# A decoder layer on one core: one key operation moved from VectorE to ScalarE, keys copied out of PSUM first, a branch and the tail's transposes placed elsewhere

## The chip, the cores and the metric

The kernel runs on one core of one Trainium2 chip. The metric is the device time of one execution in microseconds (us). The core has five engines with a queue each: PE (TensorE, matrix products and transposes), DVE (VectorE), ACT (ScalarE), POOL (GpSimd) and SP (SyncE, which here issues DMA transfers). An engine takes its instructions in the order of its own queue and waits at an instruction until what that instruction depends on is done. Matmuls write into PSUM, which has eight banks of 128 x 512 floats; DVE and ACT read them from there into SBUF.

## The reference, cut to what matters

```
h = rmsnorm(x);  proj = h @ w_in       # 512 tokens, D = 1024
# branch A: 8 heads, keys from a latent of rank 128, an indexer keeps the top 128 keys per query
o_a = sparse_attention(q_a, rmsnorm(c_kv) @ w_uk, w_uv, indexer(q_idx, k_idx, w_idx), rel_bias)
# branch B: 8 heads, stick-breaking attention
z = q_b . k_b * scale; a = exp(log_sigmoid(z) + suffix_sum(log_sigmoid(-z))); o_b = a @ v_b
x = x + (sigmoid(gate_a) * (o_a @ w_branch_a) + sigmoid(gate_b) * (o_b @ w_branch_b)) @ w_out
# 32 experts of width 256, 2 per token
h2 = rmsnorm(x); x = x + sum_e comb[:, e] * (silu(h2 @ w_gate[e]) * (h2 @ w_up[e])) @ w_down[e]
x = x + (p @ w_ple) * sigmoid(rmsnorm(x) @ w_ple_gate)
return rmsnorm(x)                      # all float32
```

## The kernel before, in words

Precision is kept by splitting: a float32 array is stored as a rounded part (hi) and a remainder (lo), and a product is three matmuls, hi·hi, lo·hi and hi·lo (`mm3`, lines L80 to L82). A weight block of 1024 columns is loaded by SP (`wraw`), rounded by POOL (`whi`, L130), and its remainder is made by DVE (`wlo`, L134).

From about 20 to 330 us the program goes through projections (`FILLS`): blocks named kb, qb (keys and queries of branch B, `kpl` and `qpl` after the copy from PSUM), qa, g (the branch gates, copied from PSUM by ACT as `gst`, L443), and the up-projections uk and uv. Each fill is 24 matmuls into one bank of a pair (`pj`, two banks in turn). Between the fills stand pieces of attention: scores `z_ps` (L491, L493) and suffix sums (L526) of branch B, logits `lg_ps` (L575, L576) of branch A, and the indexer's selection of top keys on DVE (MAX8 and MATCH_REPLACE8, L379 and L380). The order is the order of the code, laid out by hand and placed on each engine's queue by the scheduler.

A head's keys are stored stacked by `stack_k` (L291 to L298), `ks`: 64 partitions hold the head's hi, the other 64 the same hi, for slice 0; slice 1 holds the lo on both halves. It makes four operations of 64 x 512: two copies on ACT (L294, L295) and two subtractions on DVE (L296, L297), all four read from the source. It is called once for the indexer's keys (from PSUM), for the 8 heads of branch B (from `kpl`, in SBUF), and by `a_stack` (L548 to L552) for the 8 heads of branch A, two heads a call, directly from the PSUM bank `ka_ps`. That bank belongs to the `pj` pair, so the next fill but one writes it again. The four `a_stack` calls stand at about 152, 188, 228 and 269 us; the fill that takes the bank next is the qb fill at the first and a gate fill at the last.

From 442 us the mixture of experts runs as 16 pairs of experts. For each, POOL gathers 128 token rows by an indirect DMA (`xg`), PE transposes them (L1016), ACT scales them (`xT`), and PE multiplies by gate and up weights (`gu_ps`, L1031, 16 matmuls), transposes `hid`, multiplies by the down weights (`yp`, L1054) and adds the result to the tokens (`cmb_ps`, L1065, L1066). SP loads the weights `ew` ahead (L702, L704), as their buffers come free. `overflow` (L1071) is a branch at run time: it holds the work for experts with more tokens than the slots, and is jumped over when there are none (as with these inputs). Every engine loads the count into a register, compares and jumps; the join waits for the engine's own work. In the kernel before it stands inside the last pair's gate and up product, after 8 of 16 matmuls.

From 700 us the tail multiplies the normed tokens by `w_ple_gate` (`gate_x3`, four token tiles by two halves), applies the sigmoid (`sg`), adds to `x` and normalizes; `turn_h3` transposes a tile (`h3T`).

Of the kernel before, what the change touches and what calls it, by code (L numbers as in the profile page):

```python
# [49 lines left out]
def hybrid_layer_kernel(ctx: ExitStack, tc: tile.TileContext, x, p, attn_norm, w_in, kv_norm, w_uk, w_uv,  # L50
# [25 lines left out]
    def ov(name):  # L76
        return bank(7, name)
# [213 lines left out]
    def stack_k(src, r0):  # L291
        k = att.tile([P, 2, S], F32R, tag="ks", bufs=3, name="ks")
        o0 = 64 - r0
        nc.scalar.activation(k[r0:r0 + 64, 0], src[r0:r0 + 64], AF.Copy)  # L294
        nc.scalar.activation(k[o0:o0 + 64, 0], src[r0:r0 + 64], AF.Copy)  # L295
        V.tensor_sub(k[r0:r0 + 64, 1], src[r0:r0 + 64], k[r0:r0 + 64, 0].bitcast(F32))  # L296
        V.tensor_sub(k[o0:o0 + 64, 1], src[r0:r0 + 64], k[r0:r0 + 64, 0].bitcast(F32))  # L297
        return k  # L298

    onehot = tmp("onehot")  # L300
# [247 lines left out]
    def a_stack(pr):  # L548
        ka = pj("ka_ps")
        uk = late["uk"]  # L550
        mm3(ka, [uk[:, i, pr * P:(pr + 1) * P] for i in range(2)], late["cs"])
        sa[pr] = ([stack_q(heads["qa", pr], 64 * hh) for hh in range(2)], [stack_k(ka, 64 * hh) for hh in range(2)])  # L552

    def a_bias(u):
        pr, qb = u // 4, u % 4
# [316 lines left out]
    def sm(*shape):  # L872
        small[0] += 1
        return mo.tile([P, *shape], F32, name=f"sm{small[0]}")
# [124 lines left out]
    ple_part(3, 1)  # L999


    st_ = {}

    def pair_in(i):
        g_ = xg[i % 2]
        st_[i] = {}
        st_[i]["in"] = nc.gpsimd.indirect_dma_start(out=g_, out_offset=None, in_=h2_d,  # L1007
                                     in_offset=bass.IndirectOffsetOnAxis(ap=trow[:, i:i + 1], axis=0),
                                     bounds_check=S - 1, oob_is_err=False)
        gk = g_.rearrange("s (p k) -> s k p", k=KD)  # L1010
        xT = []
        for half in range(2):
            xT.append(xp.tile([P, 4, P], F32, tag="xT", bufs=4, name="xT"))
            tp = at("xg_ps")
            for k in range(4):
                nc.tensor.transpose(tp[:, k * P:(k + 1) * P], gk[:, 4 * half + k, :], ident)  # L1016
            for k in range(4):
                kk = 4 * half + k
                nc.scalar.activation(xT[half][:, k, :], tp[:, k * P:(k + 1) * P], AF.Copy, scale=gpm[:, kk:kk + 1])  # L1019
        hT_ = mo.tile([P, S], F32R, tag="hotT", bufs=2, name="hotT")  # L1020
        V.tensor_scalar(hT_, iota_t, tokf[:, i:i + 1], None, op0=ALU.is_equal)
        st_[i].update(xT=xT, hot=hT_, y={})

    def pair_gu(i, between=None):
        xT = st_[i]["xT"]
        gu_ps = pj("gu_ps")
        for k in range(KD):
            if between and k == KD // 2:
                between()
            for e in range(2):  # L1030
                nc.tensor.matmul(gu_ps[64 * e:64 * e + 64, :], xT[k // 4][:, k % 4, 64 * e:64 * e + 64],  # L1031
                                 wq[i, k // 4][:, :, e * D + (k % 4) * 256:e * D + (k % 4 + 1) * 256], start=k == 0, stop=k == KD - 1)
        hid = mo.tile([P, 256], F32, tag="hid", bufs=2, name="hid")
        nc.scalar.activation(hid, gu_ps[:, :256], AF.Silu)  # L1034
        V.tensor_mul(hid, hid, gu_ps[:, 256:])  # L1035
        st_[i]["hid"] = hid
# [23 lines left out]
    def pair_out(i, nh, ts=range(NT)):  # L1060
        yh, yl = st_[i]["y"][nh]
        hT_ = st_[i]["hot"]
        for t in ts:
# [2 lines left out]
            nc.tensor.matmul(cp_, hT_[:, t * P:(t + 1) * P], yl, start=False, stop=True)  # L1066
            xd = x2[:, t, nh * S:(nh + 1) * S]
            V.tensor_add(xd, cp_, xd)  # L1068


    def overflow():  # L1071
        most = nc.values_load(cnti[0:1, 0:1], min_val=0, max_val=2 * S)
        with tc.If(most > CAP):  # L1073
            comb = sm(NT, NE)
            V.tensor_tensor(comb, Es[:, 0], bc(over[:, 0], NE), op=ALU.mult)
            rest = t1[:, 0].rearrange("p (t e) -> p t e", e=NE)
            V.tensor_tensor(rest, Es[:, 1], bc(over[:, 1], NE), op=ALU.mult)
            V.tensor_add(comb, comb, rest)
            work_ = slot("c", F32, "of").rearrange("p a (b c) -> p (a b) c", c=D)
            hT2, fw = work_[:, 0, :].rearrange("p (k t) -> p k t", k=KD), work_[:, 1:3, :]  # L1080
            wd_ = work_[:, 3, :]
            fws = [fw[:, b, :].rearrange("p (k f) -> p k f", k=KD) for b in range(2)]
            for t in range(NT):
                hr_ = fw[:, 0, :]
                nc.sync.dma_start(hr_, h2_d[t * P:(t + 1) * P, :])
                hrk = hr_.rearrange("s (p k) -> s k p", k=KD)
                for k in range(KD):
                    tp = at("of_ps")
                    nc.tensor.transpose(tp[:, :P], hrk[:, k, :], ident)
                    V.tensor_scalar(hT2[:, k, :], tp[:, :P], gpm[:, k:k + 1], None, op0=ALU.mult)  # L1090
                with tc.For_i(0, NE, 1) as ei:
                    yps = [at("ofy") for _ in range(2)]
                    for f in range(2):
                        for w_, src in zip(fws, (w_gate, w_up)):
                            nc.sync.dma_start(w_, src[0, bass.ds(ei, 1)].rearrange("o (p k) f -> p (o k) f", k=KD)
                                              [:, :, f * P:(f + 1) * P])
                        nc.sync.dma_start(wd_, w_down[0, bass.ds(ei, 1)].rearrange("o (k p) d -> p (o k) d", p=P)[:, f, :])
                        pp = [at("ofg"), ov("ofu")]
                        for b in range(2):
                            for k in range(KD):  # L1100
                                nc.tensor.matmul(pp[b][:, :P], fws[b][:, k, :], hT2[:, k, :],
                                                 start=k == 0, stop=k == KD - 1)
                        fh = mo.tile([P, 2, P], F32, tag="hidT", bufs=2, name="fh")[:, 0, :]
                        nc.scalar.activation(fh, pp[0][:, :P], AF.Silu)
                        V.tensor_mul(fh, fh, pp[1][:, :P])
                        for nh in range(2):
                            nc.tensor.matmul(yps[nh], fh, wd_[:, nh * S:(nh + 1) * S], start=f == 0, stop=f == 1)
                    for nh in range(2):
                        xd = x2[:, t, nh * S:(nh + 1) * S]
                        V.scalar_tensor_tensor(xd, yps[nh], comb[:, t, 0:1], xd, op0=ALU.mult, op1=ALU.add)  # L1110
                    V.tensor_copy(rest[:, :, :NE - 1], comb[:, :, 1:])
                    V.tensor_copy(rest[:, :, NE - 1:], comb[:, :, :1])
                    V.tensor_copy(comb, rest)


    wpg = {}
# [53 lines left out]
                nc.scalar.activation(xt[:, c], xt[:, c], AF.Copy, scale=s3)  # L1170
            nc.sync.dma_start(out[0, t * P:(t + 1) * P, c], xt[:, c])

    def gate_x3(t, nh):
        xt = x2[:, t, :]
        s3 = ss3[:, 1, t:t + 1]
        last_ = t == NT - 1 and nh
        for n, w in ((0, 256), (256, 256)) if last_ else ((0, S),):
            c = slice(nh * S + n, nh * S + n + w)
            gp = pj("pg_ps")[:, :w]
            for k in range(KD):  # L1180
                mm3(gp, [h3t[t][:, i, k, :] for i in range(2)], [a[:, n:n + w] for a in wpg[k, nh]], first=k == 0,
                    last=k == KD - 1)
            y = xp.tile([P, S], F32, tag="xT", bufs=4, name="sg3")[:, :w]
            nc.scalar.activation(y, gp, AF.Sigmoid, scale=ss3[:, 0, t:t + 1])  # L1184
            pin(V.tensor_mul(y, y, ple["pe"][:, t, c]))  # L1185
            pin(V.tensor_add(xt[:, c], xt[:, c], y))  # L1186
            part = ss3[:, 2, t:t + 1] if nh or n else s3
            if n:
                pin(V.tensor_tensor_reduce(out=y, in0=xt[:, c], in1=xt[:, c], scale=1.0, scalar=0.0, op0=ALU.mult,
                                           op1=ALU.add, accum_out=part))  # L1190
            else:
                nc.scalar.activation(y, xt[:, c], AF.Square, accum_out=part)  # L1192
                nc.gpsimd.tensor_tensor(xt[:, c], xt[:, c], fin[:, c], op=ALU.mult)  # L1193
            if ready:
                finish()
            if nh == 0 or last_ and n == 0:
                V.tensor_scalar(s3, s3 if nh == 0 else part, 1.0 / D, EPS if nh == 0 else s3, op0=ALU.mult, op1=ALU.add)
# [8 lines left out]
    for i in range(NPR):  # L1206
# [2 lines left out]
        load_experts(3 * i + NA + NC + NB + 3)  # L1209
        if i == last:  # L1210
            load_wpg(1)
        pair_gu(i, overflow if i == last else None)
        if i + 1 < NPR:
            pair_in(i + 1)
        if i == last - 1:
# [25 lines left out]
    pair_out(last, 1, (3,))  # L1241
    for nh in range(2):
        for t in range(NT):
            gate_x3(t, nh)
            if nh == 0 and t + 2 < NT:
                turn_h3(t + 2)
                split_wpg(1, t, "bp"[t])
    finish()
    mwb.release()
    mo.release()  # L1250
# [32 lines left out]
```

## Time and profile before

| | |
|---|---|
| median of 3 runs | 761.29 us (759.28 to 762.74) |
| profiled execution | 756.49 us, span 754.8 us |
| PE busy | 723.3 us, 96% of the span |
| DVE, ACT, POOL busy | 452.9, 292.1, 216.7 us |
| mean granted clock of PE | 0.993 |

The span runs from the first to the last instruction; the execution's own time is 1.7 us longer. PE is nearly always busy, so the few places where it waits are the ones to look for. A row of a timeline has start, duration, engine, line, operation, what it writes and reads, and in brackets how long the engine was idle before it and what it waited for. In a row of windows the figures are each engine's busy time (and instructions), then the clock granted to PE (1.00 is full speed), the DMA share and GB/s.

### The profile page before, as it was taken

What the parts mean: (1) busy time and instruction counts of PE and PEld (TensorE: products, weight loads), DVE (VectorE), ACT (ScalarE), POOL (GpSimd) and SP (SyncE); (2) the same over time, 40 slices, a digit from 0 to 9 for tenths busy, and PEclk for the clock granted to TensorE, in tenths of its full rate; (3) what the DMA queues carried; (4) which work ended last, traced back from release to release, by engine and by line L of the source; (5) the groups of instructions that cost most, each with busy time, mean ns of one, the idle gap of its engine ahead of it and who ended that gap; (6) DMA issues with size and microseconds to landing.
All of it is one profiled execution on the core that took longest, in us unless ns stands there. A gap on an engine that the chain in (4) does not pass through costs nothing. (4 is left out here: it accounts for less than half of the span.)

```text
span 754.8 us, 10213 instructions
## 1 busy us (share of the span) xinstructions
PE 723.3 (96%) x3696; PEld 506.7 (67%) x3696; DVE 452.9 (60%) x896; ACT 292.1 (39%) x657; POOL 216.7 (29%) x255
## 2 busy tenths in 40 slices
PE   5999999989999999999999999999999999998995
PEld 3889987867778778788878645444544445444885
DVE  5689999997877756326553513544555445545534
ACT  5364435535667554332212423222322222233723
POOL 3212323354462535124530221000100000217732
PEclk9999999999999999999999999999999999999999
DMA  7345332322222222287955669999999999995002
GB/s 241 93 139 159 85 85 56 98 85 84 84 71 85 70 84 85 84 239 265 367 175 230 214 225 377 410 414 410 407 411 402 406 383 412 402 364 196 1 1 111
DMA packets 89259, 160.59 MB, mean 213 GB/s; under 512 B 13497, under 2 KB 56562, under 8 KB 85106
## 3 DMA queue, kind: packets, MB, share of 16 engines
q1 hardware_dynamic: 78384, 150.78, 54.8%
q10 hardware_dynamic: 8514, 4.89, 2.2%
q0 software_dynamic: 2304, 4.20, 1.6%
q8 instruction: 31, 0.51, 0.3%
q14 instruction: 26, 0.21, 0.1%
HBM read 154.08 MB, written 9.96 MB: 217 GB/s over the span
## 5 line engine op out<-in xcount | busy, mean ns | idle before, releaser
L1031 PE MATMUL gu_ps<-ew,xT 128*64 128x512 f32 x512 | 112.9, 593 | 1.4 <-PEq L1073 1.3
L130 POOL TENSOR_SCALAR whi<-wraw 128x1024 fp32r<-128x1024 f32 (+1 forms) x51 | 56.4, 1106 | 138.7 <-issue 29.7
L1068 DVE TENSOR_TENSOR x<-cmb_ps,x 128x512 f32<-128x512 f32 x128 | 81.0, 682 | 12.5 <-PE cmb_ps L1066 12.5
L1031 PEld LDWEIGHTS gu_ps<-ew,xT 128*64 128x64 f32 x512 | 36.8, 137 | 74.2 <-issue 72.8
L134 DVE TENSOR_TENSOR wlo<-wraw,whi 128x1024 fp32r<-128x1024 f32 (+1 forms) x51 | 64.7, 1269 | 14.8 <-POOL whi L130 14.8
L1007 POOL DMA_INDIRECT xg<-h_d,trow x16 | 16.1, 1008 | 186.3 <-PE cmb_ps L1065 170.9
L1035 DVE TENSOR_TENSOR hid<-hid,gu_ps 128x256 f32<-128x256 f32 x16 | 6.8, 422 | 104.4 <-ACT hid L1034 104.4
L1054 PE MATMUL yp<-ew,hidT 128*64 128x512 f32 x256 | 58.7, 599 | 0.4 <-DVE hidT L1044 0.4
L80 PE MATMUL gate_ps<-hT_hi,whi 128*128 128x512 f32 x128 | 51.9, 405 | 2.4 <-DVE ks L297 1.8
L1065 PE MATMUL cmb_ps<-yh,hotT 128*128 128x512 f32 x128 | 53.1, 415 | 0.4 <-DVE h3T L1152 0.4
L132 ACT ACTIVATE yh<-yp,sm 128x512 fp32r<-128x512 f32 x32 | 22.0, 687 | 79.2 <-PE yp L1054 79.2
L81 PE MATMUL gate_ps<-hT_lo,whi 128*128 128x512 f32 x128 | 50.8, 397 | 0.0
L82 PE MATMUL gate_ps<-hT_hi,wlo 128*128 128x512 f32 x128 | 50.7, 396 | 0.0
L1066 PE MATMUL cmb_ps<-yl,hotT 128*128 128x512 f32 x128 | 50.4, 394 | 0.3 <-DVE yl L136 0.3
L1034 ACT ACTIVATE hid<-gu_ps 128x256 f32<-128x256 f32 x16 | 6.1, 383 | 97.3 <-PE gu_ps L1031 97.3
L1054 PEld LDWEIGHTS yp<-ew,hidT 128*64 128x64 f32 x256 | 16.9, 136 | 33.0 <-issue 28.1
L136 DVE SCALAR_TENSOR_TENSOR yl<-yp,sm,yh 128x512 fp32r<-128x512 f32 x32 | 24.0, 750 | 21.1 <-ACT yh L132 21.1
L1019 ACT ACTIVATE xT<-xg_ps,gpm 128x128 f32<-128x128 f32 x128 | 34.7, 383 | 3.8 <-PE xg_ps L1016 3.8
L583 ACT ACTIVATE px<-px,st 128x128 f32<-128x128 f32 (+3 forms) x32 | 17.8, 557 | 36.6 <-DVE st L582 36.5
L80 PEld LDWEIGHTS gate_ps<-hT_hi,whi 128*128 128x128 f32 x128 | 24.3, 190 | 9.1 <-POOL bm L562 3.6
L1065 PEld LDWEIGHTS cmb_ps<-yh,hotT 128*128 128x128 f32 x128 | 24.1, 188 | 6.9 <-issue 2.4
L82 PEld LDWEIGHTS gate_ps<-hT_hi,wlo 128*128 128x128 f32 x128 | 24.5, 191 | 5.5
(328 smaller groups left out, 1760.6 us busy)
## 6 DMA issues: line engine op xcount, KB each, us to landing
ew<-in_w_gate_dram SPq DMA_DIRECT2D x32, 1024.0 KB, 8.1
ew<-in_w_up_dram SPq DMA_DIRECT2D x32, 1024.0 KB, 8.5
ew<-in_w_down_dram SPq DMA_DIRECT2D x32, 1024.0 KB, 7.5
wraw<-in_w_in_dram SPq DMA_DIRECT2D x37, 512.0 KB, 3.7
gate_d<-gst ACTq DMA_DIRECT2D x16, 256.0 KB, 2.0
sg<-gate_d SPq DMA_DIRECT2D x16, 256.0 KB, 4.4
wraw<-in_w_out_dram SPq DMA_DIRECT2D x8, 512.0 KB, 7.3
wgraw<-in_w_ple_gate_dram SPq DMA_DIRECT2D x4, 1024.0 KB, 9.4
```

The costliest lines, as they stand in the source:

```text
L80: nc.tensor.matmul(o, lhs[0], rhs[0], start=first, stop=False)
L81: nc.tensor.matmul(o, lhs[0], rhs[1], start=False, stop=False)
L82: nc.tensor.matmul(o, lhs[1], rhs[0], start=False, stop=last)
L130: hold(nc.gpsimd.tensor_scalar(hi, raw, 1.0 if gain is None else gain, 1.0, op0=ALU.mult, op1=ALU.mult))
L134: hold(V.tensor_sub(lo, raw, hi.bitcast(F32)))
L136: hold(V.scalar_tensor_tensor(lo, raw, gain, hi.bitcast(F32), op0=ALU.mult, op1=ALU.subtract))
L1019: nc.scalar.activation(xT[half][:, k, :], tp[:, k * P:(k + 1) * P], AF.Copy, scale=gpm[:, kk:kk + 1])
L1031: nc.tensor.matmul(gu_ps[64 * e:64 * e + 64, :], xT[k // 4][:, k % 4, 64 * e:64 * e + 64], wq[i, k // 4][:, :, e * D + (k % 4) * 256:e * D ...
L1054: nc.tensor.matmul(yp[64 * e:64 * e + 64, :], hidT[:, k, 64 * e:64 * e + 64], wq[i, 2][:, e, k * D + nh * S:k * D + (nh + 1) * S], start=k ...
L1065: nc.tensor.matmul(cp_, hT_[:, t * P:(t + 1) * P], yh, start=True, stop=False)
L1066: nc.tensor.matmul(cp_, hT_[:, t * P:(t + 1) * P], yl, start=False, stop=True)
L1068: V.tensor_add(xd, cp_, xd)
```

## The change

Four edits. In `stack_k` the fourth operation, DVE's subtraction L297, becomes an ACT copy of the third one's result: the lo half is moved to the other 64 partitions instead of being computed a second time. In `a_stack` ACT first copies the whole bank `ka_ps` into an SBUF tile `kl` (128 x 512), and both heads' `stack_k` read that tile. `overflow` is called in `pair_in(0)`, behind the issue of the first gather and ahead of its transposes, and no more inside the last pair; its work tile is taken from another slot. In the tail, `turn_h3(t + 2)` and `split_wpg(1, t)` are called from within `gate_x3(t, 0)`, right behind its matmuls.

```diff
-        V.tensor_sub(k[o0:o0 + 64, 1], src[r0:r0 + 64], k[r0:r0 + 64, 0].bitcast(F32))
+        nc.scalar.activation(k[o0:o0 + 64, 1], k[r0:r0 + 64, 1].bitcast(F32), AF.Copy)
...
-        sa[pr] = ([stack_q(heads["qa", pr], 64 * hh) for hh in range(2)], [stack_k(ka, 64 * hh) for hh in range(2)])
+        kl = tmp("kl")
+        nc.scalar.activation(kl, ka, AF.Copy)
+        sa[pr] = ([stack_q(heads["qa", pr], 64 * hh) for hh in range(2)], [stack_k(kl, 64 * hh) for hh in range(2)])
...
     def pair_in(i):
...
                                      bounds_check=S - 1, oob_is_err=False)
+        if i == 0:
+            overflow()
...
-    def pair_gu(i, between=None):
+    def pair_gu(i):
...
-            if between and k == KD // 2:
-                between()
...
-            work_ = slot("c", F32, "of").rearrange("p a (b c) -> p (a b) c", c=D)
+            work_ = slot("p", F32, "of").rearrange("p a (b c) -> p (a b) c", c=D)
...
-    def gate_x3(t, nh):
+    def gate_x3(t, nh, then=None):
...
                     last=k == KD - 1)
+            if then:
+                then()
...
-        pair_gu(i, overflow if i == last else None)
+        pair_gu(i)
...
-            gate_x3(t, nh)
-            if nh == 0 and t + 2 < NT:
+            def then(t=t):
                 turn_h3(t + 2)
                 split_wpg(1, t, "bp"[t])
+
+            gate_x3(t, nh, then if nh == 0 and t + 2 < NT else None)
```

On ACT's queue this is the first `a_stack` before. A name such as ka_ps is the PSUM bank of branch A's keys, kb_ps that of the kb fill, gst a gate block on its way out; in the brackets stand the engines (or DMA queues) that an instruction waits for:

```order
L294 ACTIVATE ks<-ka_ps 64x512 [waits PE_49]
L295 ACTIVATE ks<-ka_ps 64x512
L294 ACTIVATE ks<-ka_ps 64x512 [waits DVE_49]
L295 ACTIVATE ks<-ka_ps 64x512
L294 ACTIVATE ks<-kpl 64x512
L295 ACTIVATE ks<-kpl 64x512
L401 ACTIVATE kpl<-kb_ps 128x512 [waits PE_49]
L530 ACTIVATE ba<-z_ps 128x512 [waits PE_49]
```

And this is the same place on ACT after the change:

```order
L553 ACTIVATE kl<-ka_ps 128x512 [waits PE_49]
L294 ACTIVATE ks<-kl 64x512 [waits Activation_49]
L295 ACTIVATE ks<-kl 64x512
L294 ACTIVATE ks<-kl 64x512
L297 ACTIVATE ks<-ks 64x512 [waits DVE_49]
L295 ACTIVATE ks<-kl 64x512
L297 ACTIVATE ks<-ks 64x512 [waits DVE_49]
L294 ACTIVATE ks<-kpl 64x512
L295 ACTIVATE ks<-kpl 64x512
L401 ACTIVATE kpl<-kb_ps 128x512 [waits PE_49]
L297 ACTIVATE ks<-ks 64x512 [waits DVE_49]
```

The copy out of the bank is now the first of the group, the second head's L294 no longer waits for DVE, and three copies L297 that wait for DVE stand among the others.

On PE's queue the difference at the first `a_stack`'s next user of the bank, the qb fill, is:

```order
-L80 MATMUL qb_ps<-hT_hi,whi 128x512 [waits DVE_49,PE_49,Pool_49]
-L81 MATMUL qb_ps<-hT_lo,whi 128x512
-L82 MATMUL qb_ps<-hT_hi,wlo 128x512
+L80 MATMUL qb_ps<-hT_hi,whi 128x512 [waits Activation_49,Pool_49]
+L81 MATMUL qb_ps<-hT_lo,whi 128x512
+L82 MATMUL qb_ps<-hT_hi,wlo 128x512 [waits DVE_49]
```

The fill's first matmul waited for DVE (and POOL) and now waits for ACT (and POOL); DVE is waited for at the fill's third matmul, for the weight's remainder `wlo`.

On PE's queue ahead of the first gather's transposes (xg_ps), behind the products of `p @ w_ple` (pe_ps), there stands after the change (of the branch's body only the jump past it and the join are shown):

```order
L735 MATMUL pe_ps<-wpe 128x512 [waits Activation_49]
L735 MATMUL pe_ps<-wpe 128x512
L1005 TENSOR_LOAD cnti [waits DVE_49]
L1006 COMPARE_AND_BRANCH
...
L1006 UNCONDITIONAL_BRANCH [waits PE_49]
L1065 MATMUL xg_ps<-cst_sb,xg_4316 128x128 [waits DMASW0_49,DVE_49,Activation_49]
```

The load of the count, the compare and the join are new at this place; the transposes behind them wait for the gather as before.

## Rows read from the trace of the kernel before

**Rows 1.** Page, part 1: busy time of each engine, share of the span
```profile
PE 723.3 (96%) x3696; PEld 506.7 (67%) x3696; DVE 452.9 (60%) x896; ACT 292.1 (39%) x657; POOL 216.7 (29%) x255
```

**Rows 2.** Waits of PE, 150 to 300 us: total, times, longest
```profile
PE qb_ps L80 <- DVE ks L297: 2.4, 1, 2.4
...
PE lg_ps L575 <- ACT ptT L597: 1.2, 1, 1.2
```

**Rows 3.** Timeline, first `a_stack`, 152 to 166 us
```profile
152.26 0.60 ACT L443 ACTIVATE gst<-gate_ps 128x512 f32<-128x512 f32 x1 [1.75 <-PE gate_ps L82]
...
153.23 1.39 DVE L134 TENSOR_TENSOR wlo<-wraw,whi 128x1024 fp32r<-128x1024 f32 x1
...
154.67 0.50 PE L82 MATMUL kb_ps<-hT_hi,wlo 128*128 128x512 f32 x1 [0.97 <-DVE wlo L134]
...
161.38 0.68 DVE L297 TENSOR_TENSOR ks<-ka_ps,ks 64x512 fp32r<-64x512 f32 x1
...
162.10 0.59 ACT L294 ACTIVATE ks<-ka_ps 64x512 fp32r<-64x512 f32 x1 [7.65 <-DVE ks L297]
...
165.09 0.47 PE L80 MATMUL qb_ps<-hT_hi,whi 128*128 128x512 f32 x1 [2.43 <-DVE ks L297]
```

**Rows 4.** Instructions of line L297: duration ns min/median/max, first and last start
```profile
L297 DVE TENSOR_TENSOR ks<-kpl,ks x8: 684/686/1132, 58.0 to 242.6; 64x512 fp32r<-64x512 f32 x8
L297 DVE TENSOR_TENSOR ks<-ka_ps,ks x8: 683/688/693, 161.4 to 278.6; 64x512 fp32r<-64x512 f32 x8
```

**Rows 5.** Instructions of line L295, same columns
```profile
L295 ACT ACTIVATE ks<-kpl x8: 628/630/631, 54.7 to 241.9; 64x512 fp32r<-64x512 f32 x8
L295 ACT ACTIVATE ks<-ka_ps x8: 588/592/597, 153.9 to 276.2; 64x512 fp32r<-64x512 f32 x8
```

**Rows 6.** Timeline, last `a_stack`, 271 to 280 us
```profile
271.82 0.63 ACT L287 ACTIVATE qs<-qpl 64x512 fp32r<-64x512 f32 x1 [3.38 <-PE lg_ps L576]
...
278.63 0.69 DVE L297 TENSOR_TENSOR ks<-ka_ps,ks 64x512 fp32r<-64x512 f32 x1
...
279.47 0.47 PE L80 MATMUL gate_ps<-hT_hi,whi 128*128 128x512 f32 x1 [1.80 <-DVE ks L297]
```

**Rows 7.** Windows: PE, PEld, DVE, ACT, POOL busy (instructions), granted clock, DMA
```profile
160.00:168.00 8.00, 5.57 (x33) 4.86 (x32) 7.81 (x14) 4.19 (x8) 3.43 (x5) 1.00 0.25 68
...
280.00:284.00 4.00, 4.00 (x13) 3.13 (x12) 0.89 (x3) 0.90 (x2) 0.29 (x1) 0.57 0.23 69
```

**Rows 8.** Timeline, third `a_stack`, 238 to 239 us
```profile
238.15 1.37 ACT L530 ACTIVATE ba<-z_ps 128x512 f32<-128x512 f32 x3
...
238.81 0.44 PE L491 MATMUL z_ps<-qs,ks 128*128 128x384 f32 x1
```

**Rows 9.** Windows of 50 us, same columns as rows 7
```profile
100.00:150.00 50.00, 50.00 (x252) 41.27 (x251) 48.25 (x92) 22.45 (x45) 15.70 (x23) 1.00 0.29 79
...
200.00:250.00 50.00, 49.48 (x293) 39.77 (x291) 35.93 (x85) 33.11 (x79) 22.87 (x32) 1.00 0.25 75
...
550.00:600.00 50.00, 50.00 (x242) 23.55 (x240) 25.21 (x43) 13.16 (x35) 2.96 (x3) 1.00 1.02 406
```

**Rows 10.** Timeline, the branch inside the last pair
```profile
675.84 3.60 PE L1031 MATMUL gu_ps<-ew,xT 128*64 128x512 f32 x16
...
680.79 1.51 PE L1031 MATMUL gu_ps<-ew,xT 128*64 128x512 f32 x6 [1.35 <-PEq L1073]
```

**Rows 11.** Timeline, the first gather and what stands around it
```profile
445.54 1.03 PE L1016 MATMUL xg_ps<-cst_sb,xg 128*128 128x128 f32 x8
445.74 0.60 ACT L735 ACTIVATE pe<-pe_ps 128x512 f32<-128x512 f32 x1 [1.12 <-PE pe_ps L733]
...
446.66 4.51 PE L1031 MATMUL gu_ps<-ew,xT 128*64 128x512 f32 x20
```

**Rows 12.** Waits of SP's queue, 430 to 455 us: total, times, longest
```profile
SPq L702 <- PE gu_ps L1031: 7.5, 1, 7.5
```

**Rows 13.** Waits of PE, 660 to 755 us: total, times, longest
```profile
PE h_ps L1149 <- DVE x L1068: 0.4, 1, 0.4
```

More of the change, by code (lines that the diff above doesn't have):

```diff
@@ L999, in hybrid_layer_kernel, with overflow @@
     ple_part(3, 1)
+    def overflow():
+        most = nc.values_load(cnti[0:1, 0:1], min_val=0, max_val=2 * S)
+        with tc.If(most > CAP):
+            comb = sm(NT, NE)
+            V.tensor_tensor(comb, Es[:, 0], bc(over[:, 0], NE), op=ALU.mult)
+            rest = t1[:, 0].rearrange("p (t e) -> p t e", e=NE)
+            V.tensor_tensor(rest, Es[:, 1], bc(over[:, 1], NE), op=ALU.mult)
+            V.tensor_add(comb, comb, rest)
+            work_ = slot("p", F32, "of").rearrange("p a (b c) -> p (a b) c", c=D)
+            hT2, fw = work_[:, 0, :].rearrange("p (k t) -> p k t", k=KD), work_[:, 1:3, :]
+            wd_ = work_[:, 3, :]
+            fws = [fw[:, b, :].rearrange("p (k f) -> p k f", k=KD) for b in range(2)]
+            for t in range(NT):
+                hr_ = fw[:, 0, :]
+                nc.sync.dma_start(hr_, h2_d[t * P:(t + 1) * P, :])
+                hrk = hr_.rearrange("s (p k) -> s k p", k=KD)
+                for k in range(KD):
+                    tp = at("of_ps")
+                    nc.tensor.transpose(tp[:, :P], hrk[:, k, :], ident)
+                    V.tensor_scalar(hT2[:, k, :], tp[:, :P], gpm[:, k:k + 1], None, op0=ALU.mult)
+                with tc.For_i(0, NE, 1) as ei:
+                    yps = [at("ofy") for _ in range(2)]
+                    for f in range(2):
+                        for w_, src in zip(fws, (w_gate, w_up)):
+                            nc.sync.dma_start(w_, src[0, bass.ds(ei, 1)].rearrange("o (p k) f -> p (o k) f", k=KD)
+                                              [:, :, f * P:(f + 1) * P])
+                        nc.sync.dma_start(wd_, w_down[0, bass.ds(ei, 1)].rearrange("o (k p) d -> p (o k) d", p=P)[:, f, :])
+                        pp = [at("ofg"), ov("ofu")]
+                        for b in range(2):
+                            for k in range(KD):
+                                nc.tensor.matmul(pp[b][:, :P], fws[b][:, k, :], hT2[:, k, :],
+                                                 start=k == 0, stop=k == KD - 1)
+                        fh = mo.tile([P, 2, P], F32, tag="hidT", bufs=2, name="fh")[:, 0, :]
+                        nc.scalar.activation(fh, pp[0][:, :P], AF.Silu)
+                        V.tensor_mul(fh, fh, pp[1][:, :P])
+                        for nh in range(2):
+                            nc.tensor.matmul(yps[nh], fh, wd_[:, nh * S:(nh + 1) * S], start=f == 0, stop=f == 1)
+                    for nh in range(2):
+                        xd = x2[:, t, nh * S:(nh + 1) * S]
+                        V.scalar_tensor_tensor(xd, yps[nh], comb[:, t, 0:1], xd, op0=ALU.mult, op1=ALU.add)
+                    V.tensor_copy(rest[:, :, :NE - 1], comb[:, :, 1:])
+                    V.tensor_copy(rest[:, :, NE - 1:], comb[:, :, :1])
+                    V.tensor_copy(comb, rest)
@@ L1068, in pair_out @@
             V.tensor_add(xd, cp_, xd)
[L1071 to L1078, printed above, removed]
-            work_ = slot("c", F32, "of").rearrange("p a (b c) -> p (a b) c", c=D)
[L1080 to L1113, printed above, removed]
```

## Prediction

> **What bounds the kernel now.** I read the page's busy shares first. PE has 723.3 of 754.8 us [rows 1]; the other engines are far from that, so the time is PE's work and the few stretches in which PE stands still or runs slowly. The second view is the list of PE's waits between 150 and 300 us, the stretch in which the four `a_stack` calls stand: of the six entries there the two longest are for DVE's L297, and the third, 1.2 us, is for a copy on ACT [rows 2]. The third is the timeline at these two places. At the first `a_stack` the two heads' key operations take turns on one bank: the second head's L294 on ACT stands 7.65 us until the first head's L297 on DVE is through, and the qb fill, which needs the bank, is held 2.43 us by the second head's L297 [rows 3]. The two subtractions don't take long; they stand in DVE's queue behind the indexer's selection, and DVE is full: 48.25 of 50 us in the window before [rows 9]. At the last `a_stack` the same wait is 1.80 us [rows 6]. The fourth view is the table of windows: behind that second gap PE's granted clock is 0.57 of full speed for a 4 us window [rows 7], on average between the two levels of 1.2 and 2.4 GHz. After the longer gap at 165 us it stayed at 1.00 [rows 7]. Later, in the experts' stretch, PE has 50.00 of 50 us and the DMA share is 1.02 [rows 9]: both are full.
>
> **The change part by part.** The sum is made against the profiled execution, 756.49 us (span 754.8, 1.7 outside it), which lies 4.8 us under the median of the runs, 761.29. The differences are carried over to the median.
>
> *Keys, both edits.* DVE loses 17 subtractions of 0.686 to 0.688 us [rows 4], 11.7 us of queue time; by DVE's order 5 of them (the indexer's keys, four heads of B) lie ahead of the first `a_stack`, 3.4 us. ACT gains 17 copies of 64 x 512 from SBUF, 0.630 each by its copies from `kpl` [rows 5], and 4 bank copies, 0.60 each by `gst` [rows 3]; the 16 copies L294 and L295 that read `ka_ps` at 0.592 will read SBUF at 0.630 [rows 5], 0.6 in all. Together 13.7 us, on an engine that is busy 33 of 50 us in its fullest window here [rows 9].
>
> What waits changes too. The qb fill waits for one ACT copy, which can begin when `ka_ps` is written, about where L294 began in the row before the 7.65 us wait; that is over 10 us ahead of 162.66, where PE now runs dry (165.09 less 2.43) [rows 3]. So the wait goes whole: −2.4. What is late next is ACT: `ks` of the second head is needed by `lg_ps` in the middle of the qb fill, and behind the new L297 stand L294, L295, the copy of `kb_ps` and `ba`. L297 waits for DVE's L296, which comes some 3 us earlier than now, since DVE's five dropped operations are all ahead of it and a full queue keeps what it gains. The 3.4 us also cover the 0.97 us that the kb fill waits for `wlo` [rows 3], if POOL's `whi` doesn't hold it instead: between 0 and −0.97, and I take −0.9, since DVE passes to `wlo` from other work without a pause there. At the last `a_stack` ACT's bank copy falls into the 3.38 us in which ACT waits ahead of 271.82 [rows 6], so the 1.80 us [rows 6] goes whole, and with the gap, I take it, the slow clock behind it: 4 us at 0.57 do the work of 2.3 us, −1.7; the bounds are 0 (the gap wasn't its cause, since 2.43 us at 165 us cost no clock) and −1.7. Against this, ACT's extra work can delay PE where a result of ACT is awaited closely. At the third `a_stack` PE's `z_ps` begins 0.66 us behind the start of three `ba` copies on ACT [rows 8], so another bank copy ahead of them costs up to one copy, +0.6; for the other places I allow +0.3. The bounds are 0 (DVE's lead covers it) and 13.7 (all of ACT's addition on PE's path).
> By the Trainium skill's page "ScalarE: Activation LUTs", section "Rules for kernel authors", adding and multiplying belong on VectorE and not on ScalarE, which would speak against moving L297; the rows here say otherwise for float32, 0.630 on ACT against 0.686 on DVE [rows 4, 5]. By the rule ACT's side of the sum would be dearer and the slower rival likelier; by the rows it is not.
>
> *The branch.* Inside the last pair PE's two halves are parted by 1.35 us [rows 10]: that goes. At its new place the jump stands between the `pe_ps` products and the transposes at 445.54 [rows 11]. PE works up to that point and goes on at once, so nothing hides the same 1.35 us there. ACT's last copy of `pe` ends at 446.34 and its copies of `xT` follow [rows 11], so ACT, which joins later than PE, may add up to 0.8 us more. The trace doesn't show the branch there; the bounds are 0 (the gather's landing or ACT would end later anyway) and 1.35 + 0.8 + 1.7 = 3.9, the last for a slow clock as behind the gap at 279 us. I take +1.5, so the branch as a whole comes to +0.1. For SP, the join waits until the loads issued by then have landed. SP stands 7.5 us anyway for PE's release of weight buffers at this place [rows 12], and that hides it; without that cover the next loads would be late by what the landing exceeds it.
>
> *The tail.* The code moves two `turn_h3` calls, but PE's, ACT's and POOL's orders stay; on DVE two pairs of `h3T` subtractions pass ahead of an addition to `x`. PE's waits from 660 us on are the branch's and four of 0.4 us or less, of which the longest before the tail is for `x` [rows 13]. None stands inside the tail: 0, between −0.4 and +0.4.
>
> The sum is −2.4 − 0.9 − 1.8 − 1.7 + 0.9 + 0.1 = −5.8: 750.7 us for the profiled execution, 755.5 by the median.
>
> **Does the gain arrive at the end?** What PE gains before 300 us moves all that follows only if the experts' loads move with it, since their stretch is full on both sides [rows 9]. SP's wait at 442 us is for PE [rows 12], so the stream of loads starts when PE does. I take it that it moves whole.
>
> **The rivals.**
> 1. The waits change names only. ACT holds the bank as DVE did: its new L297 waits for L296 and delays what stands behind it, or the experts' loads run at their own pace and PE's lead is spent at the first `gu_ps`. For it: the second head's `ks` still hangs on DVE's queue, and the DMA share of 1.02 [rows 9]. Against it: the copy out of the bank stands ahead of all L297s, and SP's wait is for PE. The time is then 761.3 − 0.5, about 760.8.
> 2. Half of it. The two gaps go, 4.2 us, but the slow clock stays or comes at another place, the `wlo` wait passes to POOL, and ACT takes 0.9 back: −4.2 + 0.9 + 0.1 = −3.2, 758.1.
> 3. ACT becomes the bound between 50 and 290 us. Its 13.7 us lie in the chain of `ks`, `ba` and `z_ps` that PE waits for; it decides where ACT's queue ends after PE reaches `z_ps`, as it nearly does at 238.81 [rows 8]. With the gaps and the clock gone (−6.8) and all of it on PE's path, 13.7 − 6.8 = +6.9: 768.2. Against it: the longest PE wait for ACT from 150 to 300 us is 1.2 us [rows 2], and ACT has 17 us free in its fullest 50 [rows 9].
> 4. More than the sum: no loss on ACT, the branch hidden at its new place: −2.4 − 0.9 − 1.8 − 1.7 − 1.35 = −8.2, 753.1.
>
> **How the numbers follow.** A run differs from the median by up to 2 us, and 0.5% of it, 3.8 us, is about what a measurement of this kernel can tell from no change: faster is under 757.5, slower over 765.1. The chances: the forecast 0.46 (753.5 to 757.5), rival 1 0.18, rival 2 0.17, rival 3 0.10, rival 4 0.09. Faster takes the forecast's 0.44, rival 4's 0.09 and 0.06 of rival 2, about 0.59; slower is rival 3 with little more, 0.10; the rest, 0.31, is the same. The predicted time is 755.5. The range from 749.5 to 763 leaves out rival 3 and the end of rival 4; the forecast's own range is 753.5 to 757.5.
>
> **What would show it.** In the profile after, the PE rows for qb after the first `a_stack` and for gate after the last should carry no idle time, and `kb_ps` L82 none or little; the window behind the last should be granted a clock of 1.00; ACT's wait of 7.65 us should be gone from L294 and a shorter one stand at L297. The transposes after the first gather should show a gap of 1.3 to 2 us and the last pair's products none. SP's first loads behind the branch should start with PE's release, as before. The prediction is wrong if PE's waits for ACT between 150 and 300 us grow by more than 2 us, if the clock falls behind the branch, or if PE begins the experts earlier and then waits for their loads.

## The result and the profile after

The changed kernel took 751.50 us (median of 6 runs, 750.71 to 755.23) against 759.29 us for the kernel before in the same comparison (6 runs): a ratio of 0.9907, 95% interval 0.9878 to 0.9937, so 4.8 to 9.3 us less, 7.8 by the medians. The forecast was 5.8 us less, at 755.5 us. The direction is right, and 5.8 lies in the interval. The time itself is 4.0 us under the forecast and below the forecast's own range (753.5 to 757.5); half of that is the kernel before, whose median was 761.29 in the three runs shown and 759.29 in these six. The working was right in part: one step named the wrong cause, and terms that were too small or too large made up for each other.

The busy shares, from part 1 of the page of the changed kernel, in the columns of [rows 1]:

```profile
PE 721.5 (96%) x3696; PEld 505.9 (67%) x3696; DVE 440.2 (59%) x879; ACT 305.3 (41%) x678; POOL 213.0 (28%) x255
```

DVE has 12.7 us less and ACT 13.2 us more, where the forecast had 11.7 and 13.7. PE's waits from 150 to 300 us, in the columns of [rows 2]:

```profile
PE lg_ps L577 <- ACT ptT L599: 1.7, 2, 1.2
PE z_ps L491 <- ACT ba L530: 1.3, 2, 0.8
PE gate_ps L80 <- POOL bm L564: 0.6, 2, 0.3
PE kb_ps L82 <- DVE wlo L134: 0.5, 1, 0.5
PE pT_ps L597 <- DVE st L582: 0.2, 1, 0.2
```

Both waits for L297 are gone; what is new are waits for ACT. The first `a_stack` of the changed kernel, as in [rows 3]:

```profile
153.36 0.60 ACT L553 ACTIVATE kl<-ka_ps 128x512 f32<-128x512 f32 x1 [0.40 <-PE ka_ps L82]
...
154.34 0.50 PE L82 MATMUL kb_ps<-hT_hi,wlo 128*128 128x512 f32 x1 [0.54 <-DVE wlo L134]
...
160.37 0.92 DVE L296 TENSOR_TENSOR ks<-kl,ks 64x512 fp32r<-64x512 f32 x1
...
161.33 0.63 ACT L297 ACTIVATE ks<-ks 64x512 fp32r<-64x512 f32 x1 [5.40 <-DVE ks L296]
...
162.18 0.44 PE L80 MATMUL qb_ps<-hT_hi,whi 128*128 128x512 f32 x1
...
165.96 1.36 ACT L530 ACTIVATE ba<-z_ps 128x512 f32<-128x512 f32 x3
...
166.63 0.65 POOL L478 TENSOR_SCALAR_AFFINE_SELECT ba<-ba 128x256 f32<-128x256 f32 x2 [5.88 <-ACT ba L530]
...
168.29 3.06 PE L540 MATMUL ob_ps<-ba,vb 128*64 128x512 f32 x16
...
168.64 0.29 POOL L478 TENSOR_SCALAR_AFFINE_SELECT ba<-ba 128x128 f32<-128x128 f32 x1
...
168.99 0.68 PEld L540 LDWEIGHTS ob_ps<-ba,vb 128*64 128x64 f32 x6 [0.51 <-POOL ba L478]
```

In the kernel before, the first L296, the same `ba` and the matmuls that read it were:

```profile
160.70 0.67 DVE L296 TENSOR_TENSOR ks<-ka_ps,ks 64x512 fp32r<-64x512 f32 x1
...
164.98 1.36 ACT L530 ACTIVATE ba<-z_ps 128x512 f32<-128x512 f32 x3
...
168.64 0.29 POOL L478 TENSOR_SCALAR_AFFINE_SELECT ba<-ba 128x128 f32<-128x128 f32 x1
...
171.25 2.38 PE L540 MATMUL ob_ps<-ba,vb 128*64 128x512 f32 x16
```

The bank is copied in 0.60 us at 153.36 and the qb fill starts without a pause, 2.91 us earlier than in [rows 3]. ACT now waits 5.40 us at the new L297 instead of 7.65 at L294. The price stands in the five rows from 165.96 on (PEld is PE's load of weights): `ba` starts 0.98 us later than before, and the 16 matmuls that read it take 3.06 us, where before they took 2.38. What holds them is POOL's select on `ba` (L478), which follows ACT's `ba`: its last part starts at 168.64 in both kernels, while PE arrives 2.96 us earlier than before.

The third and the last `a_stack`, beside [rows 8] and [rows 6]:

```profile
236.58 0.87 ACT L530 ACTIVATE ba<-z_ps 128x512 f32<-128x512 f32 x2
...
237.22 0.44 PE L491 MATMUL z_ps<-qs,ks 128*128 128x384 f32 x1 [0.82 <-ACT ba L530]
...
238.77 0.50 PE L491 MATMUL z_ps<-qs,ks 128*128 128x512 f32 x1 [0.48 <-ACT ba L530]
...
276.41 0.40 PE L493 MATMUL z_ps<-qs,ks 128*128 128x512 f32 x1
...
276.64 0.39 PE L80 MATMUL gate_ps<-hT_hi,whi 128*128 128x512 f32 x1
```

At the third PE waits 0.82 and 0.48 us for ACT; at the last the gate fill follows at once. The windows, in the columns of [rows 7], show the clock behind the last `a_stack`, and ahead of the first gather (for this one the kernel before is the last row):

```profile
280.00:284.00 4.00, 4.00 (x28) 3.27 (x29) 2.18 (x13) 3.41 (x10) 1.42 (x2) 1.00 0.35 118
...
438.00:442.00 4.00, 2.89 (x11) 1.35 (x10) 0.00 (x0) 1.19 (x2) 0.00 (x0) 1.00 0.74 219
...
438.00:442.00 4.00, 4.00 (x7) 1.57 (x6) 0.46 (x2) 0.60 (x1) 2.28 (x2) 0.66 0.26 63
```

28 matmuls start or run in the window that held 13 [rows 7], though not the same ones. The branch, beside [rows 10, 11], in the changed kernel's timeline of PE:

```profile
441.40 1.16 PE L1065 MATMUL xg_ps<-cst_sb,xg 128*128 128x128 f32 x8 [1.11 <-ACTq L1006]
...
671.88 7.04 PE L1078 MATMUL gu_ps<-ew,xT 128*64 128x512 f32 x32
```

The last pair's matmuls have no gap, and 1.11 us stand ahead of the first transposes. SP waits in the branch (waits of SP's queue, 425 to 455 us):

```profile
SPq L1006 <- SPq L1006: 8.0, 2, 5.5
```

To see where the time goes I set the start of the same PE instruction in each profiled execution beside the one before (difference in us; below zero is earlier):

| instruction of PE (start before) | changed | copy alone | 4th op alone | branch alone | third as before |
|---|---|---|---|---|---|
| qidx (20.79) | +0.96 | +1.22 | +2.66 | +3.58 | −0.04 |
| suffix sums (159.80) | −0.33 | +1.25 | +1.37 | +3.62 | −1.27 |
| qb fill (165.09) | −2.91 | −1.34 | +0.70 | +3.62 | −3.86 |
| z_ps (173.55) | −2.26 | −1.38 | +2.23 | +3.62 | −3.19 |
| oa_ps (235.08) | −2.26 | +3.17 | +2.22 | +3.64 | −3.14 |
| gate fill (240.19) | −0.85 | +2.88 | +3.22 | +3.65 | −3.14 |
| z_ps (276.15) | −0.88 | +5.83 | +3.15 | +3.65 | −3.20 |
| gate fill (279.47) | −2.83 | +4.95 | +2.47 | +3.66 | −5.15 |
| lg_ps (283.89) | −4.52 | +3.27 | +0.86 | +3.65 | −6.84 |
| y_ps (324.82) | −3.51 | +3.28 | +1.95 | +3.64 | −5.84 |
| xg_ps (445.54) | −4.14 | +4.02 | +1.68 | +4.89 | −4.01 |
| last cmb_ps (684.38) | −5.53 | +4.02 | +1.87 | +3.48 | −5.16 |

The first row is not the change's work: executions start the projections up to 3.6 us apart, whatever the kernel. What counts is how a column changes from one row to the next. Slow stretches of the clock stand in the columns too: the +1.53 from the qb fill to z_ps with the 4th operation alone is one (0.50 from 166.6 to 169.6 us), and so are about 1.7 of the +4.55 from z_ps to oa_ps with the copy alone (0.50 from 185.5 to 188.5 us).

From qidx to the last cmb_ps PE wins 6.5 us in the changed kernel. Some 1.7 of them, between y_ps and xg_ps, are the clock ahead of the first gather, which was 0.66 in the one execution and 1.00 in the other; that is chance (last section), so the change's own steps come to about 4.8 us. The medians differ by more, 7.8 us here and 6.6 when the changed kernel was timed again. The profiled execution before was 2.8 us faster than its median, the changed one lay on its own. A part of the difference is the clock: in the second comparison the runs' mean granted clock has a median of 0.990 before and 0.995 after the change, over 755 us an estimated 3.8 us, where the forecast had 1.7.

### The profile page after: what moved, and what is told of

Same layout as the page of the kernel before. It is cut to its first block, busy times and chain, and to the rows that moved or that the text cites. A ratio compares the mean times of both kernels' runs of the same rounds, so it can differ in the third digit from the quotient of the medians.

```text
span 749.7 us, 10220 instructions
## 1 busy us (share of the span) xinstructions
PE 721.5 (96%) x3696; PEld 505.9 (67%) x3696; DVE 440.2 (59%) x879; ACT 305.3 (41%) x678; POOL 213.0 (28%) x255
## 3 DMA queue, kind: packets, MB, share of 16 engines
q10 hardware_dynamic: 8514, 4.89, 2.2%
## 5 line engine op out<-in xcount | busy, mean ns | idle before, releaser
L80 PE MATMUL gate_ps<-hT_hi,whi 128*128 128x512 f32 x128 | 51.1, 399 | 0.6 <-POOL bm L564 0.6
L80 PEld LDWEIGHTS gate_ps<-hT_hi,whi 128*128 128x128 f32 x128 | 24.0, 188 | 6.9 <-POOL bm L564 1.4
```

Source lines behind the costliest of these rows:

```text
L80: nc.tensor.matmul(o, lhs[0], rhs[0], start=first, stop=False)
```

## The experiments

Each was timed in several rounds against the kernel before on the same chip (before: median 758.11 in the first four, 759.66 in the next four, 759.56 in the last two).

| kernel | median us | ratio | interval |
|---|---|---|---|
| both key edits | 753.03 | 0.9925 | 0.9907 to 0.9943 |
| 4th operation alone | 754.98 | 0.9946 | 0.9927 to 0.9966 |
| bank copy alone | 758.85 | 1.0014 | 0.9991 to 1.0037 |
| branch alone | 758.50 | 1.0005 | 0.9988 to 1.0022 |
| changed kernel again | 753.04 | 0.9906 | 0.9873 to 0.9940 |
| third a_stack as before | 751.51 | 0.9882 | 0.9842 to 0.9921 |
| copy, 4th on ACT for A only | 756.03 | 0.9973 | 0.9942 to 1.0004 |
| copy, 4th on ACT for the others only | 758.62 | 0.9969 | 0.9938 to 0.9999 |
| tail alone | 759.50 | 0.9989 | 0.9959 to 1.0019 |
| third as before, half of the fourth | 751.15 | 0.9873 | 0.9827 to 0.9919 |

**Both key edits**, branch and tail as before:

```diff
-        V.tensor_sub(k[o0:o0 + 64, 1], src[r0:r0 + 64], k[r0:r0 + 64, 0].bitcast(F32))
+        nc.scalar.activation(k[o0:o0 + 64, 1], k[r0:r0 + 64, 1].bitcast(F32), AF.Copy)
...
+        kl = tmp("kl")
+        nc.scalar.activation(kl, ka, AF.Copy)
```

> The two key edits alone (fourth operation on ACT, bank copied to SBUF first); branch and tail as before. My theory, that the gain is made by the keys: 5.5 us less than before (5 to 7), the 2.43 and 1.80 us waits of PE gone, 1.3 us of new waits for ba on ACT at the third a_stack. Rival, that moving the branch makes part of the gain (its 1.35 us gap gone, and a slow clock of 1.5 us ahead of the first gather gone): 3 to 4 us less than before here.

It gave 5.7 us less (4.3 to 7.1), and PE's waits are the changed kernel's, row by row, but for 0.6 us at `kb_ps` where that has 0.5. The keys make the gain.

**The fourth operation alone** (the first two lines of that diff):

> Only the fourth key operation goes from DVE to ACT, the bank is still read by both heads' operations directly. My theory, that the bank's release is what counts: the last reader of the bank is then L296 instead of L297, one subtraction of 0.69 us earlier for each head, so PE's two waits shrink to about 1 us each but stay; 1.5 to 3.5 us less than before. Rival, that DVE's relief of 11.7 us is what counts: the whole gain of the keys, 5 to 6 us less.

The two waits shrank by one subtraction each, as expected, though the first stayed well above 1 us. PE's waits in that kernel:

```profile
PE qb_ps L80 <- DVE ks L296: 1.8, 1, 1.8
PE lg_ps L575 <- ACT ptT L597: 1.6, 2, 1.2
PE z_ps L491 <- ACT ba L530: 1.2, 1, 1.2
PE gate_ps L80 <- DVE ks L296: 1.1, 1, 1.1
```

2.43 became 1.76 and 1.80 became 1.12. The time fell by 4.1 us (2.6 to 5.5), more than I gave it and less than the rival's 5 to 6; the interval reaches into both, so the total doesn't decide between them. In the trace both have a part: the two waits give 1.35 us, and from qidx to the suffix sums PE wins 1.29, as in the changed kernel. Against that PE loses 1.00 at the third `a_stack` and 1.09 behind the last.

**The bank copy alone** (the last two lines, both heads reading `kl`):

> Only the copy of the bank to SBUF is added; the fourth operation stays on DVE. My theory: both PE waits for the bank go as with both edits, the 0.97 us wait for wlo stays, and ACT has 17 copies less than with both edits, so fewer of the new waits for ba: 4.5 to 6 us less than before. Rival, that DVE's relief counts: under 1.5 us less.

This is the run that refuted me: nothing gained (ratio 1.0014), though both waits for the bank are gone. PE's waits in that kernel:

```profile
PE pT_ps L597 <- DVE st L582: 4.8, 2, 2.4
PE lg_ps L577 <- ACT ptT L599: 2.6, 1, 2.6
PE kb_ps L82 <- DVE wlo L134: 1.0, 1, 1.0
```

They have moved to `pT_ps`, the transposes of the softmax row, and the wait of `lg_ps` at 185 us has grown from 1.2 to 2.6. The same kernel's DVE timeline at the third `a_stack` says why, and the PE row under it what it costs:

```profile
233.40 0.68 DVE L296 TENSOR_TENSOR ks<-kl,ks 64x512 fp32r<-64x512 f32 x1
234.10 0.69 DVE L297 TENSOR_TENSOR ks<-kl,ks 64x512 fp32r<-64x512 f32 x1
234.80 0.69 DVE L296 TENSOR_TENSOR ks<-kl,ks 64x512 fp32r<-64x512 f32 x1
235.50 1.43 DVE L297 TENSOR_TENSOR ks<-kl,ks 64x512 fp32r<-64x512 f32 x1
236.96 0.15 DVE L584 TENSOR_SCALAR st<-st 128x1 f32<-128x1 f32 x1
...
237.78 0.55 PE L597 MATMUL pT_ps<-cst_sb,px 128*128 128x128 f32 x3 [2.42 <-DVE st L582]
```

With the bank no longer passed from head to head, DVE's queue has all four subtractions in a row, 3.5 us, ahead of the softmax's `st`. In the kernel before the second head's pair stood behind it:

```profile
234.95 0.13 DVE L582 TENSOR_SCALAR st<-st 128x1 f32<-128x1 f32 x1
...
237.63 0.69 DVE L296 TENSOR_TENSOR ks<-ka_ps,ks 64x512 fp32r<-64x512 f32 x1
```

Taking away one wait let the scheduler put more work in front of another.

**The branch alone:**

> Only the branch is moved to the first gather. My theory: the 1.35 us gap leaves the last pair, 1.1 us stands ahead of the first transposes: within 0.5 us of before. Rival, that the new place avoids the slow clock in the products ahead of the first gather: 1.5 to 2 us less than before, with a clock of 1.00 between 436 and 444 us.

The ratio is 1.0005 (0.9988 to 1.0022). In the table of starts it loses 1.25 us between y_ps and xg_ps and wins 1.41 by the last cmb_ps. The rival is out: the total doesn't fall, and between 440 and 444 us the clock granted in this execution was 0.57.

**The changed kernel again, and with the third `a_stack` as before:**

```diff
+        kl = ka
+        if pr != 2:
+            kl = tmp("kl")
+            nc.scalar.activation(kl, ka, AF.Copy)
```

(and the fourth operation on DVE for those two heads).

> The changed kernel again, beside the three that follow: 6.5 to 7.5 us less than before.

> The changed kernel, with the third a_stack (heads 4 and 5) done as before: keys read from the bank, fourth operation on DVE. My theory, that PE's two new waits there, 0.82 and 0.48 us for ba, come from ACT's five added operations ahead of ba: both go, 1.0 to 1.5 us less than the changed kernel. Rival, that DVE's two subtractions are then late for the softmax (as with the copy alone): a wait of 1 to 2.4 us of pT_ps for DVE comes back at this place and the time is the same or up to 1 us more.

The changed kernel again took 0.9906 of before, as the first time. With the third as before PE's waits for `ba` shrink to one:

```profile
PE z_ps L494 <- ACT ba L533: 0.2, 1, 0.2
```

In the table of starts the step from oa_ps to the third's gate fill is +1.41 in the changed kernel and 0.00 here. So the price of the change at this place is 1.4 us, and it comes back by leaving both edits out there: with the keys read from the bank, DVE isn't late. What that takes off ACT ahead of `ba` is three operations, the bank copy and the two moved ones, and not five. Of the 1.4 us, 1.00 comes with the moved operations without the copy (the column of the 4th operation alone). By the medians it is 751.51 against 753.04 us; the two intervals overlap, so the total alone would not show it.

**Copy with the fourth operation on ACT for a part of the heads:**

```diff
+    def stack_k(src, r0, move=False):
...
+        if move:
+            nc.scalar.activation(k[o0:o0 + 64, 1], k[r0:r0 + 64, 1].bitcast(F32), AF.Copy)
```

> Bank copied, and the fourth operation moved to ACT for branch A's 8 heads alone; the indexer's keys and branch B's heads keep it on DVE; branch and tail as before. If the relief of DVE at each a_stack counts (two subtractions, 1.37 us, in front of the softmax there): 4 to 5.5 us less than before, the waits of pT_ps at 238 and 280 us gone. If the lead that DVE wins ahead of 152 us counts (3.4 us from the other keys): under 2.5 us less, with the wait of 2.6 us of lg_ps at 185 us as with the copy alone.

> Bank copied, and the fourth operation moved to ACT for the indexer's keys and branch B's 8 heads alone; branch A's heads keep it on DVE. If the relief at each a_stack counts: within 2 us of before, the waits of pT_ps at 238 and 280 us as with the copy alone. If the lead ahead of 152 us counts: 3 to 5 us less than before.

The totals, 2.0 and 2.4 us less, don't tell them apart (0.9973 and 0.9969, both at the edge of 1). With A's heads alone the total fits the second forecast and the waits fit the first; with the others alone the total lies between the two. The traces say more. With A's heads alone PE's waits for `pT_ps` sum to 0.2 us; with the others alone they are:

```profile
PE pT_ps L600 <- DVE st L585: 4.9, 3, 2.4
PE lg_ps L580 <- ACT ptT L602: 1.3, 1, 1.3
```

So the wait of `pT_ps` is decided at each `a_stack`, by A's own subtractions. The others' part lies elsewhere: from qidx to the suffix sums at 159.80 PE wins 1.27 us with the others moved and 0.03 with A's alone.

**The tail alone** (the last part of the change, `gate_x3` and its calls):

> Only the tail's edit: the two turn_h3 calls behind the matmuls of gate_x3. My theory, that PE waits nowhere in the tail: within 0.5 us of before, and PE's last matmul as far behind its first in the tail as before. Rival, that the h3T subtractions were late and the edit gives part of the gain: 1 us or more less.

No difference: the matmuls L80 of the tail start between 700.4 and 746.3 us, before between 700.3 and 746.2. The total alone would leave room for 1 us (0.9959 to 1.0019). This kernel's first `a_stack` is the one before, with the same gap of 2.40 us ahead of the qb fill, and here the clock did fall behind it, in the columns of [rows 7]:

```profile
168.50:171.30 2.80, 2.80 (x9) 2.12 (x8) 2.73 (x6) 0.21 (x1) 2.80 (x6) 0.50 0.00 0
```

**Third as before, half of the fourth** (in the fourth `a_stack` the second head's operation is on DVE again):

> As the changed kernel with the third a_stack done as before, and in the fourth a_stack the second head's fourth operation on DVE again (the bank copy stays). If ACT's load is what makes lg_ps wait 0.46 us for ptT at 288 us: that wait goes or shrinks, 0.3 to 1 us less than with the third alone changed back. If DVE is the tighter engine there: a wait of PE for DVE of 0.7 us or more comes between 275 and 290 us, and the time is the same or up to 1 us more.

The 0.46 us wait of `lg_ps` at 288 us is gone, and no new one came:

```profile
PE lg_ps L582 <- ACT ptT L604: 1.2, 1, 1.2
PE gate_ps L80 <- POOL bm L569: 0.6, 2, 0.3
PE kb_ps L82 <- DVE wlo L134: 0.6, 1, 0.6
```

From lg_ps at 283.89 to y_ps PE now gives back 0.35 us, where the changed kernel gives back 1.01. At 0.9873 of before this is the fastest kernel of the study, though its lead over the changed one (0.9907 and 0.9906) rests on the trace's steps and is not shown by the intervals.

## Why the prediction was right, point by point

- **The qb wait goes whole, −2.4.** It went: −2.58 between the suffix sums and the qb fill. The cause that the step gave, one ACT copy that releases the bank, is only half of the matter. The copy alone gained nothing, since DVE's four subtractions in a row then held the softmax. The full DVE queue stood in my first paragraph; I used it for `wlo` and not for what the copy would set free. It takes both: the copy frees the bank, and the moved operation keeps two subtractions out of the way.
- **`wlo`, −0.9.** Measured −0.43 (0.97 to 0.54 us). The step counted on a lead of 3.4 us on DVE that a full queue keeps. The first head's L296 starts 0.33 us earlier (160.37 against 160.70), or 1.29 with the later start of 0.96 taken off. Where the rest of the 3.4 us went is not shown. A part that the step didn't have came earlier: PE won 0.82 us between qidx and the z_ps at 84 us, and by the two split kernels (0.78 and 0.00 there) that belongs to the keys of the indexer and of branch B.
- **The gap at the last `a_stack`, −1.8, and the clock behind it, −1.7.** −1.95 and −1.69 in the table of starts. The clock's share is a matter of chance, see the last section. The sum put the clock behind the first gap, at 165 us, at nothing, because it had stayed at 1.00 there in the one trace; with the tail alone the same gap was followed by 0.50. So the change takes away a chance of a slow stretch at that place too.
- **ACT's lateness, +0.9.** This term was mis-sized: 0.65 at `ob_ps` (from the qb fill to z_ps), 1.41 at the third `a_stack` and 1.01 behind the last, 3.1 us together. I saw the third place and priced one copy there; three operations were added, and the kernel with the third as before shows the price of the place as a whole. Behind the last, 0.66 goes with one moved operation (1.01 to 0.35). At `ob_ps` ACT's part is argued: what PE waited for is POOL, which waited for ACT. PE's waits for ACT between 150 and 300 us grew from 1.2 to 3.0 us, just short of the 2 us that were to show the prediction wrong.
- **The branch, +0.1.** −1.52 at the last pair and +1.27 at the new place in the starts, where PE stands 1.11 us, so −0.25; by the times of the branch alone, 0. The gap is shorter than the 1.3 to 2 us that were to show it, and PE waited there for ACT's queue, the later join that the step allowed for. One sign did not come: SP's next loads did not start with PE's release. SP stood in the join itself, 8.0 us in two waits. So its cover was thinner than said: the next loads were issued at 448.20, 5.6 us behind the start of the first `gu_ps` (442.63); before, it was 3.7 us (450.35, and 446.66 in [rows 11]). PE waited for none of these loads, so the 1.9 us cost nothing.
- **The tail, 0**, and **the gain moves through the experts**: the lead of 4.14 us at xg_ps stood at 3.96 ahead of the last pair's second half, at 5.48 behind it, where the branch's gap is gone, and at 5.53 at the last cmb_ps, and PE's tail starts 5.5 us earlier from its first to its last matmul. The span is 5.1 us shorter; 0.4 are lost behind PE's last matmul.
- **The rivals.** "The waits change names only" is what the bank copy alone does, though by DVE and not by ACT. ACT as the bound did not come, but what its work delays is 3.1 of its 13.7 us, more than a fifth. By its number alone the measured 7.8 us less is nearest to rival 4 (8.2), but that rival's reasons, no loss on ACT and a hidden branch, did not come.

The Trainium skill's page "ScalarE: Activation LUTs", section "Rules for kernel authors", says to use VectorE and not ScalarE for adding and multiplying. By itself the operation was not dearer as a copy on ACT (median 0.631 us there, 0.686 as a subtraction on DVE), so the trace does not bear the rule out here for the price of one operation. The place decided: moving it cost PE 1.00 us at the third `a_stack` and won 1.29 ahead of the first, where DVE was full.

## What to carry to other kernels

Releasing a buffer early pays only if the engine behind it has room: before taking away a wait, look at what the scheduler will put in its place on the next full queue. Work is moved between engines place by place and not by a helper's line: here the steps of the trace give back 1.4 us when both edits are left out at the third `a_stack`, and another 0.7 when one operation is left on DVE at the fourth. A part of a change whose total lies within the noise can still be priced by the start of the same instruction in two traces.

## What the runs showed of the hardware that was not expected

The granted clock of PE drops to 0.50, the lower of its two levels, for a stretch of some us, at a cost of about 1.5 to 1.7 us each time, in some executions of a kernel and not in others. Ahead of the first gather it fell in 7 of the 12 profiled executions, and the changed kernel is in both groups (1.00 in the profile above, 0.67 between 436 and 440 us in the second one). Behind the last `a_stack` it fell in 4 of the 5 executions in which PE had stood 1.8 us or longer shortly before, and in none of the other 7. Over 150 to 300 us as a whole PE stood twelve times for 1.76 to 2.63 us, and eight of these were followed by such a stretch; it came nowhere else there, and the changed kernel, whose longest stand there is 1.2 us, has none. So the clock's 1.7 us in the sum is a chance that a gap gives and the change takes away, not a fixed price.

Ahead of 21 us it fell in six of the twelve, and these start the projections 2.0 to 3.6 us later than the kernel before; the others start within 1.3 us of it, but for one at 3.2 whose cause is open.

Runs of one kernel differ in the same way: the changed kernel ran in 751.28 us at a mean clock of 0.998 and in 755.23 at 0.993. These two runs have no trace of their own, so that such stretches make the difference is argued. In its two profiled executions the lower mean goes with more of them: 0.996 with none ahead of 740 us, 0.993 with two.
